# The feed-forward's first projection by Strassen's scheme

## The chip, the cores and the metric

One core of a Trainium2 chip runs the whole program as one launch. The metric is the device time in microseconds (us). The engines are TensorE (PE, which multiplies matrices into PSUM; PEld is its weight load), VectorE (DVE), ScalarE (ACT), GpSimd (POOL) and SyncE (SP, which issues nearly all DMAs). Each takes its own instructions in a fixed order; semaphores hold one engine for another.

## The reference

Two transformer blocks follow each other on 1024 tokens of width 1024. Only the second one's feed-forward is touched, with the step just ahead of it:

```
x = x + merged @ w_out
h2 = rmsnorm(x, g_ffn)
u = causal_dwconv(h2 @ w_up, conv_w, conv_b)        # w_up: 1024 x 5632, three taps over tokens
x = x + (gelu(u[..., :2816]) * u[..., 2816:]) @ w_down
ple_gate = sigmoid(rmsnorm(x, g_ple) @ w_ple_gate)
x = x + ple_gate * (p @ w_ple_up)
```

All is float32. The feed-forward's width of 2816 is 22 tiles of 128 features, each a gate tile i and a value tile i + 22.

## The kernel before

Activations lie with features on the 128 partitions and tokens along the row. A float32 product is made of three passes: each factor is split into a high part (rounded to the PE's fp32r format) and a low part, and high by high, high by low and low by high are added up in PSUM (`mm3`, line 223 for every matmul). Weights come in by SP's queue, ACT copies the high part, DVE subtracts it for the low part (`split`, lines 271 and 272); `weight` keeps two raw tiles and four of each part.

`merge` ends with `product(j, f)`, one output tile f of half j of the tokens (512 each): 24 matmuls, then DVE adds the residual (line 1821). After the third tile of the second half, `norm(0)` normalises the first half: squares on ACT, their sum mostly on POOL (line 448), a root by small matmuls, then for each of 8 tiles a scaling on DVE (line 475), the high part (477) and the low part (478). `norm(1)` does the same at the end.

`ffn` takes the 22 activations in groups of 4, 4, 4, 4 and 6. For one activation, `ffn_act` multiplies the gate and the value tile of `w_up` with both halves, 48 matmuls into two PSUM banks each; ACT scales straight from PSUM by the last tap (line 1933), DVE adds the two other taps, again from PSUM (line 1936), ACT takes gelu (1938), POOL multiplies (1939), and the product is split. It stays in SBUF. After each group `down` adds that group's share of all 8 output tiles into `xacc` (line 1858), while the next group's first activation is prepared. Then the last stage multiplies by `w_ple_gate`.

The order of instructions on each engine is chosen by the framework's scheduler: by the order of the program, filled up with what its own cost estimates say is ready.

Of the kernel before, what the change touches and what calls it, by code (L numbers as in the profile page):

```python
# [17 lines left out]
P = 128  # L18
# [19 lines left out]
FF_GROUPS = (4, 4, 4, 4, 6)  # L38
# [178 lines left out]
class _Builder:  # L217
# [123 lines left out]
    def build(self):  # L341
        nc, tc, a = self.nc, self.tc, self.a
        with ExitStack() as es:
# [1442 lines left out]
    def merge(self):  # L1786
# [4 lines left out]
        with tc.tile_pool(name="merge", bufs=1, reuse_waits="tile") as pool:  # L1791
# [21 lines left out]
            for j, t in enumerate(half):  # L1813
                X = self.hp.tile([P, KT, 512], F32, tag="h", name="x")
                nc.sync.dma_start(out=X, in_=src[:, t].rearrange("(k p) t -> p k t", p=P))
                xs.append(X)
            def product(j, f):
# [3 lines left out]
                nc.vector.tensor_tensor(out=xs[j][:, f, :], in0=ps, in1=xs[j][:, f, :], op=ALU.add)  # L1821

            def norm(j):
                t = half[j]
                if self.stop == "m":
                    self.store(a["out"][:, t].rearrange("(k p) t -> p k t", p=P), xs[j])
                self.store(dst[:, t].rearrange("(k p) t -> p k t", p=P), xs[j])
                h = self.h_tiles(512)
                self.norm(pool, xs[j], 512, lambda f: self.vec("g_ffn", f), None, h[0], h[1])
                hs.append(h)  # L1830

            for f in range(KT):
                product(0, f)
            for f in range(KT):
                product(1, f)
                if f == 2:
                    norm(0)
            norm(1)
        return hs

    def ffn(self, hs):
        nc, tc, a = self.nc, self.tc, self.a
        with tc.tile_pool(name="ffn", bufs=1, reuse_waits="tile") as big:
            X = big.tile([P, KT, SEQ], F32, name="xacc")
            for j in range(2):
                nc.sync.dma_start(out=X[:, :, 512 * j:512 * j + 512], in_=self.xd[0][:, 512 * j:512 * j + 512].rearrange("(k p) t -> p k t", p=P))
# [19 lines left out]
            with tc.tile_pool(name="ffa", bufs=1, reuse_waits="tile") as pool:  # L1866
                u_t = self.hp.tile([P, 4, SEQ], F32, tag="h", name="u")
                act = lambda i: self.ffn_act(pool, hs, i, u_t[:, 2 * (i % 2):2 * (i % 2) + 2])
                first, acts = 0, []
                for gn in FF_GROUPS:  # L1870
                    acts += [act(first + i) for i in range(len(acts), gn)]
                    ahead = [act(first + gn)] if first + gn < FFT else []
                    weight = lambda f: self.weight(a["w_down"][f][:, first * P:(first + gn) * P])
                    if ahead:
                        for f in range(KT):
                            w = weight(f)
                            for j in range(2):
# [78 lines left out]
```

## Time and profile before

| | us |
|---|---|
| median of 3 runs | 4063.01 (4056.43 to 4072.8) |
| the profiled execution | 4071.35 |
| its span | 4069.6 |
| PE busy | 3755.1 |
| DVE busy | 2386.8 |
| ACT busy | 1612.1 |
| POOL busy | 929.7 |

The feed-forward runs from about 3211 to 3950 us of the span. A matmul's recorded 0.39 us overlaps with the next one's, so PE's pace is read from how many start in a window, not from the mean of one.

### The profile page before, as it was taken

What the parts mean: (1) busy time and instruction counts of PE and PEld (TensorE: products, weight loads), DVE (VectorE), ACT (ScalarE), POOL (GpSimd) and SP (SyncE); (2) the same over time, 40 slices, a digit from 0 to 9 for tenths busy, and PEclk for the clock granted to TensorE, in tenths of its full rate; (3) what the DMA queues carried; (4) which work ended last, traced back from release to release, by engine and by line L of the source; (5) the groups of instructions that cost most, each with busy time, mean ns of one, the idle gap of its engine ahead of it and who ended that gap; (6) DMA issues with size and microseconds to landing.
All of it is one profiled execution on the core that took longest, in us unless ns stands there. A gap on an engine that the chain in (4) does not pass through costs nothing. (4 is left out here: it accounts for less than half of the span.)

```text
span 4069.6 us, 52648 instructions
## 1 busy us (share of the span) xinstructions
PE 3755.1 (92%) x18392; PEld 2809.5 (69%) x18392; DVE 2386.8 (59%) x5500; ACT 1612.1 (40%) x3251; POOL 929.7 (23%) x1127
## 2 busy tenths in 40 slices
PE   5899999888899999799999989989869999999999
PEld 4755666566755666478778866666648788888877
DVE  5888755645787747655664337776544543434354
ACT  4445663334346653543333234443343422222243
POOL 3233322311233324311110023343312100000020
PEclk8999999989999999899999978998879999999999
DMA  5111126564111135543333242121224411111133
GB/s 179 46 43 42 55 88 188 188 215 147 39 42 40 56 129 191 166 129 89 108 100 102 87 115 55 47 69 23 68 100 143 149 50 47 50 47 47 49 92 105
DMA packets 267890, 379.20 MB, mean 93 GB/s; under 512 B 56400, under 2 KB 145440, under 8 KB 264024
## 3 DMA queue, kind: packets, MB, share of 16 engines
q1 hardware_dynamic: 267624, 375.83, 29.8%
q8 instruction: 146, 2.39, 0.3%
q14 instruction: 120, 0.98, 0.1%
HBM read 280.90 MB, written 87.54 MB: 91 GB/s over the span
## 5 line engine op out<-in xcount | busy, mean ns | idle before, releaser
L223 PE MATMUL pp<-h,wh 128*128 128x512 f32 (+1 forms) x1696 | 527.3, 388 | 50.6 <-DVE x L1148 16.9
L223 PE MATMUL pp<-wh,h 128*128 128x384 f32 (+1 forms) x1792 | 518.2, 352 | 15.4 <-ACT v L548 12.6
L272 DVE TENSOR_TENSOR wl<-wr,wh 128x512 fp32r<-128x512 f32 (+3 forms) x386 | 299.7, 781 | 393.4 <-ACT wh L271 391.6
L223 PE MATMUL dd<-h,wh 128*128 128x512 f32 x1664 | 519.5, 393 | 0.0
L271 ACT CAST wh<-wr 128x512 fp32r<-128x512 f32 (+3 forms) x386 | 249.9, 651 | 611.3 <-PE pp L223 286.7
L223 PEld LDWEIGHTS pp<-h,wh 128*128 128x128 f32 x1696 | 315.7, 194 | 128.9 <-ACT wh L271 17.8
L709 POOL TENSOR_TENSOR acc<-acc,p 128x512 f32<-128x512 f32 (+3 forms) x246 | 295.3, 1200 | 443.3 <-ACT p L694 275.7
L223 PEld LDWEIGHTS dd<-h,wh 128*128 128x128 f32 x1664 | 312.5, 188 | 71.4 <-DVE h L478 0.3
L223 PEld LDWEIGHTS pp<-wh,h 128*128 128x128 f32 x1792 | 335.2, 194 | 34.0 <-ACT v L548 13.9
L223 PE MATMUL rp<-h,side 128*128 128x512 f32 x1440 | 350.6, 396 | 0.0
L223 PE MATMUL pp<-h,wl 128*128 128x512 f32 (+1 forms) x848 | 327.1, 386 | 1.0 <-DVE wl L272 0.9
L223 PE MATMUL dd<-h,wl 128*128 128x512 f32 x832 | 325.9, 392 | 0.0
L223 PE MATMUL pp<-wl,h 128*128 128x384 f32 (+1 forms) x896 | 312.6, 349 | 0.0
L223 PE MATMUL sp<-q,k 66*128 66x512 f32 (+6 forms) x944 | 300.1, 407 | 11.2 <-DVE p L692 5.7
L223 PEld LDWEIGHTS rp<-h,side 128*128 128x128 f32 x1440 | 266.5, 189 | 52.0
L634 DVE TENSOR_REDUCE mx<-mp 128x1 f32<-128x512 f32 (+1 forms) x472 | 250.7, 559 | 55.3 <-PE mp L223 53.4
L223 PE MATMUL mp<-k,q 128*128 128x512 f32 (+3 forms) x664 | 232.5, 383 | 13.5 <-DVE mx L634 6.4
L709 DVE TENSOR_TENSOR acc<-acc,p 128x512 f32<-128x512 f32 (+3 forms) x246 | 201.1, 817 | 68.0 <-ACT p L694 26.8
L223 PEld LDWEIGHTS sp<-q,k 128*128 128x128 f32 (+1 forms) x944 | 164.0, 192 | 108.7 <-issue 55.7
L694 ACT ACTIVATE p<-sp 128x512 f32<-128x512 f32 (+1 forms) x316 | 181.4, 594 | 141.3 <-PE sp L223 128.1
L223 PE MATMUL pp<-act,wh 128*128 128x512 f32 x704 | 221.4, 396 | 2.0 <-ACT act L271 1.1
L223 PE MATMUL vp<-p,v 128*64 128x512 f32 (+3 forms) x824 | 212.9, 596 | 5.5 <-ACT p L694 5.1
(371 smaller groups left out, 6705.5 us busy)
## 6 DMA issues: line engine op xcount, KB each, us to landing
wr<-in_w_out SPq DMA_DIRECT2D x96, 256.0 KB
wr<-in_w_up SPq DMA_DIRECT2D x88, 256.0 KB
wmod<-in_w_mod SPq DMA_DIRECT2D x16, 1024.0 KB
wr<-in_w_tok SPq DMA_DIRECT2D x40, 384.0 KB
xd<-x SPq DMA_DIRECT2D x6, 2048.0 KB
wr<-in_w_feat SPq DMA_DIRECT2D x40, 256.0 KB
bq<-in_na_bias SPq DMA_DIRECT2D x16, 640.0 KB
yd<-yr SPq DMA_DIRECT2D x32, 256.0 KB
```

Of the source, the lines that this page charges most:

```text
L223: return self.nc.tensor.matmul(out, lhsT=lhsT, rhs=rhs, start=start, stop=stop)
L271: self.nc.scalar.copy(out=hi, in_=src)
L272: self.nc.vector.tensor_tensor(out=lo, in0=src, in1=hi.bitcast(F32), op=ALU.subtract)
L634: nc.vector.tensor_reduce(out=m, in_=ps[:, :n], axis=AX.X, op=ALU.max)
L694: made = nc.scalar.activation(out=p[:, j, :n], in_=st[:, :n], func=AF.Exp)
L709: u.summed = eng.tensor_tensor(out=u.acc[:, j, q0:q0 + n], in0=u.acc[:, j, q0:q0 + n], in1=p[:, j, :n], op=ALU.add)
```

## The change

One gate and one value tile, with both halves of the inner dimension, form a 2 x 2 block matrix; the two halves of the features and of the tokens form the other. The four block products of 128 by 512 by 512 each have two terms, eight multiplications; the change makes seven, by Winograd's form of Strassen's scheme. It needs sums of blocks on both sides:

- The tokens' side, once: `norm_here` scales both halves in place, and `turn_b` forms four difference blocks t1 to t4 on DVE and POOL, each split. `merge` now adds up the squares as the tiles come, alternately on DVE and POOL, spreads the first half's norm over the second half's products, and stores the residual by ACT's queue.
- The weights' side, per pair: `blocks` loads both tiles and makes four sums on POOL; `operand` splits each of the seven operands, four products ahead.
- The results: `tile_pair` adds the seven products up, partly from PSUM on DVE, partly on POOL, into z in SBUF; the convolution reads z from there. Its steps are laid out by a table of product numbers, and from product 14 on the order is kept as written (`pin`).

PSUM is one ring of eight banks in this stage. All 22 activations are written to DRAM by ACT's queue and read back by SP's queue for `down`, which now has groups of 4 and six times 3; the last two groups run for the first half of the tokens, then for the second.

```
-FF_GROUPS = (4, 4, 4, 4, 6)
+FF_GROUPS = (4, 3, 3, 3, 3, 3, 3)
+PIN = 14
+AHEAD = 4
...
+    def pin(self, op):
+        return (lambda **k: self.tc.keep_in_program_order(op(**k))) if self.pinned else op
...
-            with self.weights("second"), self.psum("dense", pp=2, tp=1, vp=1, dd=2):
-                hs = self.merge()
-                if self.stop == "m":
-                    return
-                self.ffn(hs)
+            with tc.tile_pool(name="factor", bufs=1) as fp:
+                with self.weights("second"), self.psum("merge", pp=2, tp=1, vp=1):
+                    hs = self.merge(fp)
+                    if self.stop == "m":
+                        return
+                with self.psum("up", pp=8):
+                    self.up(*hs)
+            with tc.tile_pool(name="x", bufs=1, reuse_waits="tile") as xp, self.weights("third"):
+                with self.psum("dense", pp=2, tp=1, vp=1, dd=2):
+                    self.ffn(xp.tile([P, KT, SEQ], F32, name="xacc"))
...
+    def norm_here(self, X, gain, r, first, hi, lo, fs):
+        for f in fs:
+            self.nc.vector.scalar_tensor_tensor(out=X[:, f], in0=X[:, f], scalar=gain(f), in1=r, op0=ALU.mult, op1=ALU.mult)
+            if f >= first:
+                self.split(X[:, f], hi[:, f - first], lo[:, f - first])
...
+            sums, here = [None, None], self.norm_tile(pool)
+            tile = lambda tag: fp.tile([P, 512], F32, tag=tag, name=tag) if tag == "nr" else here(tag)
...
+                nc.scalar.dma_start(out=(a["out"] if self.stop == "m" else dst)[f * P:(f + 1) * P, half[j]], in_=xs[j][:, f])
+            def add(j, f):
+                sums[j] = self.norm_sum(xs[j], 512, nc.gpsimd if f % 2 else nc.vector, tile, (f,), sums[j])
...
+                    t = self.hp.tile([P, 2, 4, 512], F32R, tag="h", name="h22")
+                    h = [t[:, 0], t[:, 1]]
...
+                r = self.norm_root(pool, sums[j], 512, tile)
+                return [lambda f=f: self.norm_here(xs[j], lambda k: self.vec("g_ffn", k), r, 4 * j, *h, range(f, f + 2)) for f in ((0, 2, 4, 6) if j == 0 else (4, 6, 0, 2))]
...
+                if f == 1:
+                    todo = norm(0)
+                elif todo:
+                    todo.pop(0)()
+                if f >= 3:
+                    for k in range(4) if f == 3 else (f,):
+                        add(1, k)
+            last = norm(1)
+        return hs, xs, last
...
+            def diff(eng, t, k, out, x, y):
+                eng.tensor_tensor(out=out, in0=x, in1=y, op=ALU.subtract)
+                self.split(out, t[0][:, k], t[1][:, k])
+            def turn_b():
+                x0, x1 = ([X[:, k] for k in range(KT)] for X in xs)
+                for k in range(4):
+                    diff(V, t1, k, x0[k], x1[k], x0[k])
+                for k in range(4):
+                    G.tensor_tensor(out=x1[k], in0=x1[k + 4], in1=x1[k], op=ALU.subtract)
+                    diff(V, t2, k, x1[k + 4], x1[k + 4], x0[k])
+                for k in range(4):
+                    self.split(x1[k], t3[0][:, k], t3[1][:, k])
+                    diff(G, t4, k, x0[k + 4], x0[k + 4], x1[k + 4])
+            z_t = self.hp.tile([P, 4, SEQ], F32, tag="h", name="z")
+            act_t = self.hp.tile([P, 2, 2, SEQ], F32R, tag="h", name="act")
+            z, u = z_t[:, 0:2], z_t[:, 2:4]
+            left, right = slice(0, 512), slice(512, 1024)
+            held = lambda: pool.tile([P, 512], F32, tag="held", name="held", bufs=4)
...
+            def blocks(i):
+                raw = []
+                for s in range(2):
+                    t = pool.tile([P, 2, 512], F32, tag="raw", name="raw", bufs=4)
+                    nc.sync.dma_start(out=t.rearrange("p k c -> p (k c)"), in_=a["w_up"][i + FFT * s])
+                    raw += [t[:, 0], t[:, 1]]
+                a11, a12, a21, a22 = raw
+                s1, s2 = (pool.tile([P, 512], F32, tag="sum", name="sum", bufs=4) for _ in range(2))
+                self.pin(G.tensor_tensor)(out=s1, in0=a21, in1=a22, op=ALU.add)
+                self.pin(G.tensor_tensor)(out=s2, in0=s1, in1=a11, op=ALU.subtract)
+                self.pin(G.tensor_tensor)(out=a21, in0=a11, in1=a21, op=ALU.subtract)
+                s4 = lambda: self.pin(G.tensor_tensor)(out=a12, in0=a12, in1=s2, op=ALU.subtract)
+                return [a11, a12, s1, s2, a21, a22, a12], s4
...
+            def lower():
+                src, t = operand.last
+                ins = self.pin(V.tensor_tensor)(out=t[:, 1], in0=src, in1=t[:, 0].bitcast(F32), op=ALU.subtract)
+                operand.done = operand.done[0], ins
...
+            order = [(0, 0), (0, 1), (1, 0), (1, 1), (0, 6), (1, 6)]
+            order += [(i, j) for i in range(FFT) for j in range(7) if (i, j) not in order]
+            got = {}
+            def operand(n):
+                if n < len(order):
+                    i, j = order[n]
+                    if i not in got:
+                        got[i] = blocks(i)
+                    if j == 5 and i >= 1 and i + 1 < FFT:
+                        got[i + 1] = blocks(i + 1)
+                    src = got[i][0][j]
+                    t = pool.tile([P, 2, 512], F32R, tag="op", name="op", bufs=6)
+                    copied = self.pin(A.copy)(out=t[:, 0], in_=src)
+                    operand.done = copied, operand.done[1]
+                if n and n <= len(order):
+                    if n != AHEAD:
+                        lower()
+                    i, j = order[n - 1]
+                    if j == 1:
+                        got[i][1]()
+                if n < len(order):
+                    operand.last = src, t
+                    ops.append(t)
...
+            of_b = (b11, b21, t1, t2, t3, t4, b22)
+            def product(n):
+                operand(n + AHEAD)
+                b, w, ps = of_b[order[n][1]], ops.pop(0), self.bank()
+                for k in range(4):
+                    c = slice(k * P, (k + 1) * P)
+                    for i, (x, y) in enumerate(((0, 0), (0, 1), (1, 0))):
+                        self.mm(ps, w[:, x, c], b[y][:, k], k + i == 0, k == 3 and i == 2)
+                return ps
...
+            def convolve(i, s):
+                self.pin(A.activation)(out=u[:, s], in_=z[:, s], func=AF.Identity, scale=taps(i, s)(2), bias=self.vec("conv_b", i + FFT * s))
+                def rest():
+                    for n in (1, 0):
+                        d = 2 - n
+                        self.pin(V.scalar_tensor_tensor)(out=u[:, s, d:], in0=z[:, s, :SEQ - d], scalar=taps(i, s)(n), in1=u[:, s, d:], op0=ALU.mult, op1=ALU.add)
+                return rest
...
+            def tile_pair(i):
+                add = lambda eng, out, x, y: self.pin(eng.tensor_tensor)(out=out, in0=x, in1=y, op=ALU.add)
+                act, b, at, rest = act_t[:, i % 2], made[i], {}, {}
+                p, v, uv = held(), held(), held()
+                def put(n, fn):
+                    at.setdefault(n, []).append(fn)
+                put(1, lambda: self.pin(A.copy)(out=p, in_=b[0]))
+                put(2, lambda: add(V, z[:, 0, left], b[1], p))
+                put(3, lambda: self.pin(A.copy)(out=v, in_=b[2]))
+                put(4, lambda: add(V, p, b[3], p))
+                put(4, lambda: add(G, uv, p, v))
+                put(5, lambda: add(V, p, b[4], p))
+                put(5, lambda: add(G, z[:, 1, right], p, v))
+                put(6, lambda: add(V, z[:, 1, left], b[5], p))
+                put(7, lambda: add(V, z[:, 0, right], b[6], uv))
+                put(7, lambda: rest.update(x=convolve(i, 1)))
+                put(8, lambda: rest["x"]())
+                put(8, lambda: rest.update(y=convolve(i, 0)))
+                put(9, lambda: rest["y"]())
+                put(10, lambda: self.pin(A.activation)(out=u[:, 0], in_=u[:, 0], func=AF.Gelu_apprx_tanh))
+                put(11, lambda: self.pin(G.tensor_tensor)(out=u[:, 0], in0=u[:, 0], in1=u[:, 1], op=ALU.mult))
+                put(13, lambda: self.pin(A.copy)(out=act[:, 0], in_=u[:, 0]))
+                put(14, lambda: self.pin(V.tensor_tensor)(out=act[:, 1], in0=u[:, 0], in1=act[:, 0].bitcast(F32), op=ALU.subtract))
+                put(15, lambda: self.pin(nc.scalar.dma_start)(out=self.ad[i], in_=act.bitcast(F32)))
+                first = 7 * i + 4
+                todo.extend((first + n, fn) for n in sorted(at) for fn in at[n])
...
+            with tc.issue_after(operand.done[0].ins), tc.issue_after(operand.done[1].ins):
+                for fn in norm:
+                    fn()
+                turn_b()
+            for n, (i, j) in enumerate(order):
+                self.pinned = n >= PIN
+                if j == (2 if i < 2 else 0):
+                    tile_pair(i)
+                made[i][j] = product(n)
+                run(n)
...
+                if i % 2 == 0:
+                    t = self.hp.tile([P, 2, 2, SEQ], F32R, tag="h", name="acts")
+                nc.sync.dma_start(out=t[:, i % 2].bitcast(F32), in_=self.ad[i])
+                self.acts.append(t[:, i % 2])
...
+                def load(i):
+                    t = pool.tile([P, 2, SEQ], F32R, tag="act", name="act", bufs=6)
+                    nc.sync.dma_start(out=t.bitcast(F32), in_=self.ad[i])
+                    return t
+                starts = [sum(FF_GROUPS[:n]) for n in range(len(FF_GROUPS))]
+                weight = lambda n, f: self.weight(a["w_down"][f][:, starts[n] * P:(starts[n] + FF_GROUPS[n]) * P])
+                acts = {0: self.acts}
+                for n in range(len(FF_GROUPS) - 2):
+                    acts[n + 1] = []
+                    for f in range(KT):
+                        w = weight(n, f)
+                        if n == 0:
+                            nc.sync.dma_start(out=X[:, f], in_=self.xd[0][f * P:(f + 1) * P, 0:SEQ])
+                        if f % 2 and f // 2 < FF_GROUPS[n + 1]:
+                            acts[n + 1].append(load(starts[n + 1] + f // 2))
+                        for j in range(2):
+                            down(acts[n], w, f, j, range(FF_GROUPS[n]))
+                todo = []
+                for j in range(2):
+                    for n in (-2, -1):
+                        n += len(FF_GROUPS)
                         for f in range(KT):
-                            w = weight(f)
-                            for j in range(2):
-                                down(acts, w, f, j, range(gn))
-                    else:
-                        w = [weight(f) for f in range(2)]
-                        for ks in (range(gn - 1), range(gn - 1, gn)):
-                            for f in range(2):
-                                down(acts, w[f], f, 0, ks)
-                        for f in range(2, KT):
-                            down(acts, weight(f), f, 0, range(gn))
-                        todo = norm(0)
-                        for f in range(KT):
-                            w = weight(f)
+                            w = weight(n, f)
+                            if j == 0 and n + 1 < len(FF_GROUPS) and f % 2 and f // 2 < FF_GROUPS[n + 1]:
+                                acts.setdefault(n + 1, []).append(load(starts[n + 1] + f // 2))
                             if todo:
                                 todo.pop(0)()
-                            down(acts, w, f, 1, range(gn))
-                    first += gn
-                    acts = ahead
+                            down(acts[n], w, f, j, range(FF_GROUPS[n]))
...
-    def ffn_act(self, pool, hs, i, u):
```

## Rows read from the trace of the kernel before

**Rows 1.** The page's header, busy times and slices of the span.
```profile
span 4069.6 us, 52648 instructions
...
PE 3755.1 (92%) x18392; PEld 2809.5 (69%) x18392; DVE 2386.8 (59%) x5500; ACT 1612.1 (40%) x3251; POOL 929.7 (23%) x1127
...
PE   5899999888899999799999989989869999999999
...
PEclk8999999989999999899999978998879999999999
```

**Rows 2.** Windows: stretch, us, PE, PEld, DVE, ACT, POOL busy (instructions), PEclk, DMA share, GB/s.
```profile
3150.00:3200.00 50.00, 46.25 (x204) 37.59 (x203) 27.93 (x44) 19.57 (x32) 9.08 (x6) 0.97 0.35 116
...
3300.00:3350.00 50.00, 50.00 (x218) 40.72 (x217) 23.25 (x27) 12.21 (x16) 4.79 (x2) 1.00 0.18 51
...
3850.00:3900.00 50.00, 48.03 (x201) 38.21 (x199) 21.00 (x22) 16.67 (x21) 7.77 (x4) 0.97 0.25 72
```

**Rows 3.** Timeline of PE in merge: start, us, engine, line, operation, idle before.
```profile
3192.70 0.77 PE L223 MATMUL pp<-m21h,wh 128*128 128x512 f32 x1 [3.75 <-ACT h L477]
...
3194.12 0.63 PE L223 MATMUL pp<-m21h,wh 128*128 128x512 f32 x1
3194.55 0.63 PE L223 MATMUL pp<-m21l,wh 128*128 128x512 f32 x1
```

**Rows 4.** Groups by line and shape, 3000 to 4070: count, busy us, mean ns, idle, releasers.
```profile
L272 DVE TENSOR_TENSOR wl<-wr,wh 128x512 fp32r<-128x512 f32 x196 | 142.2, 727 | 263.9 <-ACT wh L271 263.6
...
L271 ACT CAST wh<-wr 128x512 fp32r<-128x512 f32 x196 | 121.1, 619 | 402.2 <-PE dd L223 196.8 <-PE pp L223 173.9 <-DMA wr<-in_w_out 14.4
...
L1936 DVE SCALAR_TENSOR_TENSOR u<-dd,vecs,u 128x1023 f32<-128x1023 f32 x44 | 56.5, 1283 | 21.6 <-ACT u L1933 21.5
...
L1858 DVE TENSOR_TENSOR xacc<-pp,xacc 128x512 f32<-128x512 f32 x80 | 55.2, 691 | 117.0 <-PE pp L223 116.9
L1933 ACT ACTIVATE u<-dd,vecs 128x1024 f32<-128x1024 f32 x44 | 52.9, 1202 | 1.9 <-PE dd L223 1.9
L1939 POOL TENSOR_TENSOR u<-u 128x1024 f32<-128x1024 f32 x22 | 52.6, 2392 | 622.1 <-DVE u L1936 602.2 <-DMA wr<-in_w_down 20.0
...
L272 DVE TENSOR_TENSOR act<-u,act 128x1024 fp32r<-128x1024 f32 x22 | 27.0, 1226 | 67.9 <-ACT act L271 67.9
...
L271 ACT CAST act<-u 128x1024 fp32r<-128x1024 f32 x22 | 23.1, 1049 | 98.7 <-POOL u L1939 98.7
...
L475 DVE SCALAR_TENSOR_TENSOR y<-x,vecs,nr 128x512 f32<-128x512 f32 x16 | 11.1, 746 | 3.9 <-ACT nr L462 3.9
```

**Rows 5.** Timelines of POOL, then of DVE, where both work.
```profile
3191.37 1.72 POOL L448 TENSOR_TENSOR nrb<-nrb,y 128x512 f32<-128x512 f32 x1 [34.58 <-ACT y L446]
3193.83 4.95 POOL L448 TENSOR_TENSOR nrb<-nrb,y 128x512 f32<-128x512 f32 x3 [0.74 <-ACT y L446]
3203.26 1.29 POOL L448 TENSOR_TENSOR nrb<-nrb,y 128x512 f32<-128x512 f32 x1 [4.49 <-ACT y L446]
...
3329.47 2.40 POOL L1939 TENSOR_TENSOR u<-u 128x1024 f32<-128x1024 f32 x1 [20.31 <-DVE u L1936]
```
```profile
3191.87 0.68 DVE L1821 TENSOR_TENSOR x<-pp,x 128x512 f32<-128x512 f32 x1
...
3194.76 2.87 DVE L272 TENSOR_TENSOR wl<-wr,wh 128x512 fp32r<-128x512 f32 x2
...
3330.86 1.57 DVE L272 TENSOR_TENSOR wl<-wr,wh 128x512 fp32r<-128x512 f32 x1
```

**Rows 6.** Timeline of DVE from merge's last addition to the second norm's first scaling.
```profile
3211.01 0.69 DVE L1821 TENSOR_TENSOR x<-pp,x 128x512 f32<-128x512 f32 x1
3212.42 0.69 DVE L272 TENSOR_TENSOR wl<-wr,wh 128x512 fp32r<-128x512 f32 x1 [0.72 <-ACT wh L271]
...
3218.53 2.08 DVE L475 SCALAR_TENSOR_TENSOR y<-x,vecs,nr 128x512 f32<-128x512 f32 x3 [1.93 <-ACT nr L462]
```

**Rows 7.** Windows in which two 2 MB loads move.
```profile
3230.00:3235.00 5.00, 5.00 (x24) 4.10 (x23) 3.73 (x4) 2.74 (x4) 0.00 (x0) 1.00 1.04 376
```

More of the change, by code (lines that the diff above doesn't have):

```diff
@@ L1784, in rwkv, with merge @@
                         nc.sync.dma_start(out=a["out"][f * P:(f + 1) * P, 256 * j:256 * j + 256], in_=o)
-    def merge(self):
+    def merge(self, fp):
         nc, tc, a = self.nc, self.tc, self.a
@@ L1827, in norm @@
-                self.store(dst[:, t].rearrange("(k p) t -> p k t", p=P), xs[j])
-                h = self.h_tiles(512)
-                self.norm(pool, xs[j], 512, lambda f: self.vec("g_ffn", f), None, h[0], h[1])
+                if j == 0:
+                    h = self.h_tiles(512)
+                else:
+                    t = self.hp.tile([P, 2, 4, 512], F32R, tag="h", name="h22")
+                    h = [t[:, 0], t[:, 1]]
                 hs.append(h)
+                r = self.norm_root(pool, sums[j], 512, tile)
@@ L1832, in merge @@
+                return [lambda f=f: self.norm_here(xs[j], lambda k: self.vec("g_ffn", k), r, 4 * j, *h, range(f, f + 2)) for f in ((0, 2, 4, 6) if j == 0 else (4, 6, 0, 2))]
             for f in range(KT):
                 product(0, f)
+                add(0, f)
+            todo = []
             for f in range(KT):
                 product(1, f)
[L1836 to L1841, printed above, removed]
+                if f == 1:
[5 more added lines that the diff above has]
+                        add(1, k)
@@ new lines, in merge, with up, taps, run @@
+            last = norm(1)
+        return hs, xs, last
+    def up(self, hs, xs, norm):
+        nc, tc, a = self.nc, self.tc, self.a
+        V, G, A = nc.vector, nc.gpsimd, nc.scalar
+        self.pinned = False
+        self.ad = self.dp.tile([FFT, P, 2, SEQ], F32, name="ad")
+        with tc.tile_pool(name="up", bufs=1, reuse_waits="tile") as pool:
+            def diff(eng, t, k, out, x, y):
[16 more added lines that the diff above has]
+            held = lambda: pool.tile([P, 512], F32, tag="held", name="held", bufs=4)
+            ts = {n: pool.tile([P, 2, 4, 512], F32R, name="t%d" % n) for n in (4, 3)}
+            def blocks(i):
[11 more added lines that the diff above has]
+                return [a11, a12, s1, s2, a21, a22, a12], s4
+            ops = []
+            def lower():
[25 more added lines that the diff above has]
+                    ops.append(t)
+            operand.done = None, None
+            for n in range(AHEAD):
+                operand(n)
+            lower()
+            ts.update({n: pool.tile([P, 2, 4, 512], F32R, name="t%d" % n) for n in (1, 2)})
+            b11, b21, b22 = [x[:, 0:4] for x in hs[0]], [x[:, 4:8] for x in hs[0]], hs[1]
+            t1, t2, t3, t4 = ([ts[n][:, 0], ts[n][:, 1]] for n in range(1, 5))
+            of_b = (b11, b21, t1, t2, t3, t4, b22)
[7 more added lines that the diff above has]
+                return ps
+            def taps(i, s):
+                return lambda n: self.vec("conv_w", 2 * FFT * n + i + FFT * s)
+            def convolve(i, s):
[5 more added lines that the diff above has]
+                return rest
+            todo = []
+            def run(n):
+                for x in [x for x in todo if x[0] <= n]:
+                    todo.remove(x)
+                    x[1]()
+            def tile_pair(i):
[24 more added lines that the diff above has]
+                todo.extend((first + n, fn) for n in sorted(at) for fn in at[n])
+            made = [[None] * 7 for _ in range(FFT)]
+            with tc.issue_after(operand.done[0].ins), tc.issue_after(operand.done[1].ins):
[8 more added lines that the diff above has]
+                run(n)
+            self.acts = []
+            for i in range(FF_GROUPS[0]):
+                if i % 2 == 0:
+                    t = self.hp.tile([P, 2, 2, SEQ], F32R, tag="h", name="acts")
+                nc.sync.dma_start(out=t[:, i % 2].bitcast(F32), in_=self.ad[i])
+                self.acts.append(t[:, i % 2])
+            for n in range(len(order), len(order) + 24):
+                run(n)
@@ L1893, in ffn @@
-                    first += gn
-                    acts = ahead
+                            down(acts[n], w, f, j, range(FF_GROUPS[n]))
+                    if j == 0:
+                        todo = norm(0)
             if self.stop == "f":
```

34 lines of the change are left out of this document (2 added, 32 removed).

## The prediction

> **What bounds the kernel now.** I read the page's busy table and slices first: TensorE (PE) is busy 92% of a 4069.6 us span, and in the last quarter of the slices it is full but for a tenth here and there, at a clock of 9 tenths or more [rows 1]. The windows say it harder: across the feed-forward a 50 us window holds 50.00 us of PE, 218 matmuls and clock 1.00, while VectorE (DVE) is busy 23 us, ScalarE (ACT) 12 and GpSimd (POOL) 5 [rows 2]. So this stage runs at PE's pace, 50 / 218 = 0.229 us per matmul of 512 columns, and only two places lose some: 3150 to 3200 (PE 46.25, clock 0.97) and 3850 to 3900 (48.03, 0.97). The first is a wait of 3.75 us of PE behind the norm of the first half, followed by matmuls at 0.43 us apart for some 3 us, that is at 1.2 GHz [rows 3]. Every other engine is hidden under PE here. The question is whether that still holds when PE's work shrinks by an eighth and that of DVE and POOL grows.
>
> **What is removed.** The up-projection has 44 tiles of 48 matmuls, 2112 x 0.229 = 483.6 us. Afterwards it has 154 block products of 12, 1848 x 0.229 = 423.2 us: 60.4 us of PE go. The down-projection keeps its 22 x 8 x 2 x 3 = 1056.
>
> **What is added per pair of tiles** (one pair of gate and value tiles gives seven products; PE needs 84 x 0.229 = 19.2 us). Durations are from [rows 4]:
> - DVE: 7 low parts of operands, 0.69 each where POOL is idle [rows 6], 4.8; 5 additions of a product from PSUM at 0.69, 3.5; 4 convolution taps of 1023 columns at 1.28, 5.1; the low part of the activation 1.23. Sum 14.6 us (before: four low parts, four taps, one 1.23, 9.1).
> - POOL: 4 sums of weight blocks and 2 of products at 1.29 [rows 5], 7.7, and the gating product 2.39. Sum 10.1 us (before 2.4).
> - ACT: 9 copies at 0.62, 2 scalings at 1.20, gelu and high part taken at 1.05 each. Sum 10.1 us; hidden.
>
> Alone, each lies below 19.2. But DVE and POOL don't run beside each other freely. In [rows 5] POOL multiplies from 3329.47 to 3331.87; a DVE low part that starts at 3330.86 takes 1.57 us where 0.69 is usual and ends 0.56 us after POOL. Two of them at 3194.76 take 2.87 us under three POOL additions, which themselves take 1.65 each for 1.29. Yet a DVE addition that takes one input from PSUM keeps its 0.68 under a running POOL addition (3191.87). What shuts the other out is two SBUF inputs. Now the change does two things at once: it multiplies POOL's work by four, and its taps read z from SBUF, where before they read PSUM; so of DVE's 14.6 us, 4.8 + 5.1 + 1.2 = 11.2 (76%) are of the kind that waits.
>
> What a POOL operation costs DVE: all but the start of both, which overlaps (0.69 - 0.56 = 0.13 us on DVE, about as much on POOL), so 1.0 us for one of 512 columns and 2.1 for the gating product (the parts that exclude one another add up to 11.2 + 10.1 - 19 x 0.13 = 18.8 us of a pair). That is 6 x 1.0 + 2.1 = 8.1 us per pair when every one meets such a DVE operation, 0.76 x 8.1 = 6.2 when they meet in proportion. DVE then needs 20.8 to 22.7 us per pair, more than PE's 19.2. Below lies only the case that they never meet, 19.2. I take 21.3: the proportion, and half a us because DVE works in order and waits for ACT (before, 67.9 us in 22 waits for the activation's high part alone [rows 4]). So DVE, not PE, sets the pace of the up-projection.
>
> The Trainium skill ("SBUF — State Buffer", section "Who interferes with whom") speaks against the change here: a DVE instruction with two SBUF inputs and a GpSimd one that reads SBUF share one lock, and the second to issue is blocked for the whole instruction. The rows agree on who blocks whom, not on the whole instruction: by that the lock alone would be held 21.3 us per pair and bind by itself (2 us a pair above PE's pace even with DVE's PSUM additions free; that the figure is the one I took is chance), while by the rows the starts overlap.
>
> **Head of the up-projection.** After merge's last matmul the chain of the second norm took 3211.01 to 3218.53 before the first scaled column, 7.5 us [rows 6]; its last addition is moved to POOL (1.29 for 0.69), so 8.1. Before, PE filled this with the first half's matmuls. Now DVE has 8 scalings at 0.746, 20 low parts and 8 differences at 0.69: 25.3 us, and 8 differences on POOL cost it some 7 more, before the last of Strassen's token blocks stands: 8.1 + 25.3 + 7 = 40.4 us. PE can do ten products in 27.5 us by then, so it is late by 13 even if nothing else binds.
>
> DVE's account to the last product: 40.4 + 22 x 21.3, less 7 low parts that fit into the chain's gaps (4.8), less what it does after the last product (additions 2.1, taps 5.1, 1.2, the gating product 2.1: 10.5) = 493.7 us, against 483.6: **+10.1**. Ends: 20.8 gives -1, 22.7 gives +41, PE's pace with the late head 423.2 + 13 gives -47.
>
> **Turn to the down-projection.** Its first four activations (4 MB) can load once the first half's tiles are free, five products (15 us) ahead of the end; two 2 MB loads moved 376 GB/s [rows 7], so 11 us: hidden. What isn't is DVE's 10.5 us rest, behind which the two PSUM banks' additions and the first weights' low parts stand. I take **+6** (0 to 15). A gap here and one at the head each end in some matmuls at half clock, as the gap in merge did [rows 3], where it cost 0.03 x 50 = 1.5 us [rows 2]: **+3**.
>
> **The down-projection.** Seven groups for five: 112 additions for 80, each 0.69 under 9 matmuls (2.06 us), and one low part of 384 columns per two of them, under the 0.73 of 512: at most 2.1 of 4.1 us, hidden by PE; uncovered it would be 32 x 0.69 = 22 us. The activations' writes go over ACT's queue, 1 MB in 21 us; the reads stand in SP's queue ahead of weights, 2.7 us per MB, and the slowest group needs 9 MB in 44 us, 205 GB/s, half of what was seen. I take **+2** (0 to 12) for weights that arrive late behind an activation that itself waits for a buffer; DVE, then PE stand behind such a weight.
>
> **What goes.** The norm of the first half is cut into steps between products, so the 3.75 us wait and its slow clock, 5 us, should go; and the last group no longer waits for the last activation, 50 - 201 x 0.229 = 4.0 us, of which I count 3.7 [rows 2]: **-8.7**. What is late next there is the second half's norm, which the head above carries. Moving the residual's stores, sixteen of 256 KB, from SP's queue to ACT's costs nothing: ACT is busy a quarter of the feed-forward's windows, and nothing waits for the stores before the down-projection.
>
> **Sum**: +10.1 + 6 + 3 + 2 - 8.7 = +12.4 on the profiled execution's 4071.35, 4084; that execution lies 8.3 above the median of the runs, 4063.01, so 4076 against that.
>
> **Rivals.** (a) PE stays the bound: the queues run far enough ahead that POOL's operations fall beside DVE's PSUM additions and gaps. For it: the 18.8 us that exclude one another fit under 19.2, operands are made four products ahead, eight PSUM banks. Against: each engine's order is fixed, and 98% use of what two engines share, with no queueing, is much to ask. -47 + 6 + 3 + 2 - 8.7 = -45: 4018. (b) Slower: every POOL operation stops DVE, in the steady part of the up-projection, because DVE is never idle and its next operation is nearly always a two-input one (12 of 17). Price 22.7 per pair, +41 for +10: 4106. From 21.6 us per pair on the whole is over 0.5% slower. For it: the two low parts under three POOL additions, where all met. Against: ACT's waits let POOL work alone at times. (c) The round trip through DRAM binds: activations wait for buffers in SP's queue, six groups lose 5 us each where I counted 2 in all: 4104. Against: 376 GB/s and a whole group of lead. That fewer products are computed than said can't be: they are counted in the code.
>
> **Chances.** About 0.5% (20 us) is what a measurement of this kernel can tell from no change. Forecast 0.42, (a) 0.31, (b) 0.22, (c) 0.05. The forecast's own range is 4052 to 4096; since (a) has a third, the whole range takes it in, down to 4010 (its sum with the turn at nothing and the reads at nothing), and reaches up almost to (b), 4104. Faster than 4043: (a) nearly whole, 0.30. Over 4083: (b), (c) all but whole and a tail of the forecast, 0.30. Between: 0.40.
>
> **What would show it.** Matmuls fall by 264. In windows of the up-projection DVE would be near 50 of 50 with low parts of a mean well over 0.69 and taps over 1.28, PE near 45, its waits ended by DVE's low parts; a new group of matmuls should begin every 21 us per pair. If PE stands at 50.00 there and DVE's taps at 1.28, (a) is right and the exclusion was overrated. If PE waits for activations or weights in the last 260 us of that stage, it is (c). The head should show PE idle 10 us or more behind low parts of token blocks.

## The result, and the profile after

The changed kernel took 4090.47 us in the median (4083.16 to 4096.25, 6 runs) against 4066.30 of the kernel before beside it (4056.43 to 4072.8, 6 runs): a ratio of 1.0067, 95% interval 1.0047 to 1.0087. It is slower by 0.7%. The rise is 24 us where 12.4 were forecast; the time lies inside the range given, above the 4083 over which the prediction had put 0.30. That range is wide, so the time alone says little for the mechanism; the rows below say more.

The page's header, busy times and two rows of slices, of the kernel after, as [rows 1] of before:

```profile
span 4093.2 us, 52895 instructions
...
PE 3702.4 (90%) x18128; PEld 2760.2 (67%) x18128; DVE 2667.7 (65%) x5756; ACT 1675.9 (41%) x3395; POOL 1184.5 (29%) x1263
...
PE   5899999888899999799999989999869799998999
...
PEclk7999999989999999899999978998979899999999
```

PE lost 264 matmuls and 53 us of work, and the span grew all the same. Windows of merge and of the up-projection, columns as in [rows 2]:

```profile
3150.00:3200.00 50.00, 50.00 (x226) 40.94 (x225) 30.98 (x49) 21.09 (x35) 5.22 (x4) 1.00 0.44 143
...
3300.00:3350.00 50.00, 47.53 (x202) 38.55 (x202) 47.18 (x40) 22.80 (x32) 31.18 (x16) 0.97 0.23 85
3450.00:3500.00 50.00, 43.60 (x185) 34.89 (x184) 47.15 (x40) 22.12 (x32) 31.92 (x16) 0.97 0.23 85
```

In merge the wait of [rows 3] is gone: PE is at 50.00 where 46.25 stood. In the up-projection, where PE filled 50 of 50 before, DVE is the engine with almost no idle time now. Groups of DVE, then of POOL, from 3300 to 3650 us (count, busy us, mean ns, idle, releaser), beside [rows 4]:

```profile
L242 DVE TENSOR_TENSOR op<-raw,op 128x512 fp32r<-128x512 f32 x81 | 100.6, 1242 | 0.0
L242 DVE SCALAR_TENSOR_TENSOR z<-z,vecs 128x1022 f32<-128x1022 f32 x33 | 72.5, 2196 | 1.2
L242 DVE SCALAR_TENSOR_TENSOR z<-z,vecs 128x1023 f32<-128x1023 f32 x32 | 57.3, 1790 | 0.0
L242 DVE TENSOR_TENSOR z<-pp,held 128x512 f32<-128x512 f32 x49 | 33.6, 685 | 1.8
L242 DVE TENSOR_TENSOR held<-pp,held 128x512 f32<-128x512 f32 x32 | 21.9, 685 | 18.9 <-POOL held L242 18.9
```
```profile
L242 POOL TENSOR_TENSOR raw<-raw 128x512 f32<-128x512 f32 x17 | 38.5, 2265 | 0.0
L242 POOL TENSOR_TENSOR sum<-raw 128x512 f32<-128x512 f32 x16 | 36.3, 2267 | 0.0
```

In the mean a low part takes 1.24 us for 0.69, a tap 2.20 or 1.79 for 1.28, a POOL sum of these two groups 2.27 for 1.29; the two groups with one input in PSUM stay at 0.685. The means mix long and short ones: of the low parts in the first row 48 take 0.68, 16 take 1.18 and 17 take 2.89, and of the taps with 1023 columns half take 1.27 and half 2.31. (The line L242 is the helper that keeps an order.) How the two engines take turns shows in their timelines, DVE first, then POOL:

```profile
3400.01 3.51 DVE L242 SCALAR_TENSOR_TENSOR z<-z,vecs 128x1023 f32<-128x1023 f32 x2
3403.44 1.77 DVE L242 TENSOR_TENSOR op<-sum,op 128x512 fp32r<-128x512 f32 x1
...
3410.98 2.88 DVE L242 TENSOR_TENSOR op<-raw,op 128x512 fp32r<-128x512 f32 x1
...
3421.50 3.51 DVE L242 SCALAR_TENSOR_TENSOR z<-z,vecs 128x1023 f32<-128x1023 f32 x2
```
```profile
3400.23 2.21 POOL L242 TENSOR_TENSOR raw<-raw,sum 128x512 f32<-128x512 f32 x1 [3.03 <-DVE op L242]
3402.40 2.26 POOL L242 TENSOR_TENSOR sum<-raw 128x512 f32<-128x512 f32 x1
...
3410.90 2.42 POOL L242 TENSOR_TENSOR z<-z 128x1024 f32<-128x1024 f32 x1 [2.31 <-ACT z L242]
```

Each ends about its own length after the other has ended: the second POOL sum ends at 3404.66, the low part that started under it ends at 3405.21, 0.55 later. The low part of 2.88 us stands under the gating product. The Trainium skill ("SBUF — State Buffer", section "Who interferes with whom") has this as a lock that whoever issues first holds for the whole instruction; the rows agree but for the start of each, some 0.14 us, which overlaps.

What PE waits for in the same stretch (us, times, longest):

```profile
PEld pp L225 <- DVE z L242: 31.2, 16, 2.6
PE pp L225 <- DVE z L242: 24.4, 16, 2.2
```

DVE's additions of products into z come late, so no PSUM bank is free for the next product. A pair takes 21.50 us on DVE once the pace is steady: the first taps of two pairs start at 3400.01 and 3421.50. By the starts of PE's products the mean from the fourth pair to the 21st is 21.24, because two of these 17 spacings, 19.04 and 19.63, are of the time before the backlog.

The stage account of all kernels, in us of each profiled execution. "Up" runs from merge's last addition on DVE to the start of the last product's last matmul; "turn" from there to the down-projection's first; "down" from there to the first matmul of the stage after. "Pair" is the steady spacing. (The kernel before alternates between up and down, so only its sum is given.)

| kernel | pair | up | turn | down | sum |
|---|---|---|---|---|---|
| before | | | | | 739.5 |
| after | 21.50 | 498.2 | 11.1 | 262.3 | 771.6 |
| e1_all_on_vector | 19.04 | 457.6 | 3.9 | 262.1 | 723.6 |
| e2_write_only | 19.04 | 454.1 | 3.8 | 261.7 | 719.5 |
| e3_sums_on_vector | 20.20 | 472.7 | 11.8 | 262.1 | 746.6 |
| e7_weight_sums_on_gpsimd | 20.18 | 473.8 | 7.6 | 261.9 | 743.3 |
| e4_last_pass_joined | 21.50 | 498.1 | 11.2 | 250.5 | 759.7 |
| e5_vector_and_joined | 19.04 | 457.5 | 3.8 | 250.5 | 711.8 |
| e6_and_token_differences | 19.04 | 453.5 | 3.7 | 250.3 | 707.6 |
| e8_six_operands_ahead | 19.04 | 448.1 | 3.7 | 250.5 | 702.3 |

From before to after these stages grow by 32.1; merge's last addition stands 8.2 earlier (3211.01 to 3202.84: the forecast's 5, and 3.4 of scatter ahead of merge), the stage after is the same within 0.4. That is the 23.6 us between the two profiled executions (4095.0 and 4071.35). Single executions scatter more than some effects below: merge's last addition stands at 3190.50 in e1 and 3204.20 in e8, with the same code up to there. So small effects are read from the stages, one trace for each kernel.

### The profile page after: what moved, and what is told of

It is laid out like the page before. It is cut to its first block, busy times and chain, and to the rows that moved or that the text cites. A ratio compares the mean times of both kernels' runs of the same rounds, so it can differ in the third digit from the quotient of the medians.

```text
span 4093.2 us, 52895 instructions
## 1 busy us (share of the span) xinstructions
PE 3702.4 (90%) x18128; PEld 2760.2 (67%) x18128; DVE 2667.7 (65%) x5756; ACT 1675.9 (41%) x3395; POOL 1184.5 (29%) x1263
## 5 line engine op out<-in xcount | busy, mean ns | idle before, releaser
L277 ACT CAST wh<-wr 128x512 fp32r<-128x512 f32 (+4 forms) x322 | 199.7, 625 | 428.0 <-PE pp L225 258.2
L278 DVE TENSOR_TENSOR wl<-wr,wh 128x512 fp32r<-128x512 f32 (+4 forms) x322 | 240.0, 751 | 192.3 <-ACT wh L277 190.1
L225 PEld LDWEIGHTS pp<-wh,h 128*128 128x128 f32 x1792 | 333.2, 193 | 35.4 <-ACT v L566 14.7
L225 PE MATMUL sp<-q,k 66*128 66x512 f32 (+6 forms) x944 | 299.1, 406 | 11.2 <-DVE p L710 5.9
L225 PE MATMUL pp<-t,op 128*128 128x512 f32 x1056 | 256.2, 402 | 41.6 <-DVE z L242 26.6
L225 PEld LDWEIGHTS pp<-t,op 128*128 128x128 f32 x1056 | 203.0, 194 | 94.1 <-DVE z L242 33.8
L225 PE MATMUL mp<-k,q 128*128 128x512 f32 (+3 forms) x664 | 231.9, 382 | 14.6 <-DVE mx L652 6.2
L459 POOL TENSOR_TENSOR nrb<-nrb,y 128x512 f32<-128x512 f32 (+1 forms) x52 | 67.7, 1302 | 501.8 <-ACT y L457 485.4
L225 PEld LDWEIGHTS mp<-k,q 128*128 128x128 f32 x664 | 119.7, 189 | 123.9 <-DVE mx L652 54.4
```

What stands on the lines that cost most here:

```text
L225: return self.nc.tensor.matmul(out, lhsT=lhsT, rhs=rhs, start=start, stop=stop)
L277: self.nc.scalar.copy(out=hi, in_=src)
L278: self.nc.vector.tensor_tensor(out=lo, in0=src, in1=hi.bitcast(F32), op=ALU.subtract)
L459: (add or (nc.vector if f == KT - 1 else nc.gpsimd)).tensor_tensor(out=rb[:, :n], in0=rb[:, :n], in1=sq[:, :n], op=ALU.add)
```

## The experiments

The theory: POOL's operations and DVE's with two SBUF inputs exclude each other, and this makes DVE the bound. e1 to e4 ran beside one set of runs of before (median 4060.21, 13 runs), e5 to e8 beside another (4061.44, 17 runs).

**e1_all_on_vector.** All seven POOL operations of a pair go to DVE, the busiest engine of the stage.

```
-self.pin(G.tensor_tensor)(out=s1, in0=a21, in1=a22, op=ALU.add)
+self.pin(V.tensor_tensor)(out=s1, in0=a21, in1=a22, op=ALU.add)
...
-put(4, lambda: add(G, uv, p, v))
+put(4, lambda: add(V, uv, p, v))
...
-put(11, lambda: self.pin(G.tensor_tensor)(out=u[:, 0], in0=u[:, 0], in1=u[:, 1], op=ALU.mult))
+put(11, lambda: self.pin(V.tensor_tensor)(out=u[:, 0], in0=u[:, 0], in1=u[:, 1], op=ALU.mult))
```

> GpSimd's seven operations per pair (four sums of weight blocks, two of products, the gating product) are given to VectorE; nothing else changes. Theory (VectorE sets the pace, and a GpSimd operation that reads SBUF costs a two-SBUF-input VectorE operation about 1.0 us of 1.29): VectorE then needs 14.6 + 6 x 0.69 + 1.23 = 20.0 us per pair, low parts back to 0.69 and taps to 1.28, against 21.24 before: 20 to 27 us less, about 4066, although the busiest engine gets 5.4 us more work per pair. Rival 1 (VectorE is simply given too much, the exclusion adds little): its busy 19.9 us per pair grows by 5.4 to 25.3, 22 x 4.1 = 89 us more, 4180. Rival 2 (the order of the queues and PSUM banks set the pace): no change, 4090.

Measured: 4041.64 us (4035.4 to 4047.94), ratio to before 0.9955 (0.994 to 0.997): 1.1% below the changed kernel's ratio, some 45 us, and below the kernel before. A window and three DVE groups of this kernel:

```profile
3300.00:3350.00 50.00, 50.00 (x223) 41.40 (x222) 48.85 (x65) 23.66 (x34) 0.00 (x0) 1.00 0.27 101
```
```profile
L242 DVE TENSOR_TENSOR op<-raw,op 128x512 fp32r<-128x512 f32 x88 | 60.2, 684 | 0.0
L242 DVE SCALAR_TENSOR_TENSOR z<-z,vecs 128x1023 f32<-128x1023 f32 x38 | 48.5, 1277 | 0.0
...
L242 DVE TENSOR_TENSOR raw<-raw,sum 128x512 f32<-128x512 f32 x17 | 11.8, 692 | 0.6
```

With seven operations more DVE is done sooner: 18.62 us busy per pair, low parts and taps back at their own length, and PE is the bound at 19.04. I had expected 20.0 for DVE from summed durations. Its operations run closer together than they last, in the timeline of this kernel 0.60 us apart at 0.68 each:

```profile
3202.34 0.68 DVE L1928 TENSOR_TENSOR raw<-raw 128x512 f32<-128x512 f32 x1
3202.95 0.68 DVE L1929 TENSOR_TENSOR raw<-raw,sum 128x512 f32<-128x512 f32 x1
3203.55 0.68 DVE L1936 TENSOR_TENSOR op<-raw,op 128x512 fp32r<-128x512 f32 x1
```

**e2_write_only.** Each POOL operation becomes two memsets of the same tile, so that POOL stays busy but reads nothing. The sums, the gating product and with them the values are left out.

```
+w = lambda out: [self.pin(G.memset)(ap=out, constant=0.01) for _ in range(2)]
...
-self.pin(G.tensor_tensor)(out=s1, in0=a21, in1=a22, op=ALU.add)
+w(s1)
...
-put(4, lambda: add(G, uv, p, v))
+put(4, lambda: w(uv))
```

> Each of GpSimd's seven operations per pair is replaced by two memsets of the same output tile, so GpSimd still works but reads nothing; the sums, the gating product and with them the values are left out. Theory (what excludes is GpSimd reading SBUF beside a VectorE operation with two SBUF inputs): low parts at 0.69, taps at 1.28, TensorE's 19.2 us per pair sets the pace, about 41 us less, 4050. Rival 1 (any GpSimd activity holds VectorE up): low parts and taps stay well above that in proportion to GpSimd's busy time, and the pace stays above 20.5. Rival 2 (VectorE's own 14.6 us and its waits in order set the pace): durations fall, the pace stays near 21.

Measured: 4037.58 us (2 runs), ratio 0.9945 (0.9925 to 0.9965). A window, and one group each of POOL and DVE:

```profile
3300.00:3350.00 50.00, 50.00 (x222) 41.38 (x222) 35.05 (x45) 23.89 (x33) 19.78 (x34) 1.00 0.29 106
```
```profile
L242 POOL MEMSET raw<- 128x512 f32 x61 | 32.1, 527 | 106.9 <-DVE op L242 105.2
```
```profile
L242 DVE TENSOR_TENSOR op<-raw,op 128x512 fp32r<-128x512 f32 x80 | 55.2, 690 | 68.4 <-ACT op L242 68.4
```

POOL is still busy 20 us of 50, and DVE's low parts stay at 0.69 and its taps at 1.28. They do meet: here a low part starts under a memset that runs until 3400.63, and keeps its 0.69.

```profile
3399.68 0.95 POOL L242 MEMSET z<- 128x1024 f32 x1
```
```profile
3400.41 0.69 DVE L242 TENSOR_TENSOR op<-raw,op 128x512 fp32r<-128x512 f32 x1 [1.43 <-ACT op L242]
```

So it is POOL's reading that holds DVE, not its being busy. The Trainium skill ("SBUF — State Buffer", section "Who interferes with whom") has this too: two SBUF inputs contend with a GpSimd instruction that reads SBUF, not with one that only writes it. DVE's own work of a pair, measured bare here, is 13.88 us. The stages fall by 52 us where 41 were expected for the pace: up by 44, the turn by 7.

**e3_sums_on_vector.** Only the four weight sums go to DVE (the edit of e1, `s1`, `s2`, `a21` and `s4` alone).

> Only the four sums of weight blocks per pair go from GpSimd to VectorE; the two sums of products and the gating product stay. Theory: VectorE 14.6 + 4 x 0.69 = 17.4, plus 0.76 x (2 x 1.0 + 2.1) = 3.1 for what GpSimd still does: 20.5 us per pair, 0.75 x 22 = 16 us less than the changed kernel, 4074. Rival (too much on VectorE): 19.9 + 2.8 = 22.7 per pair, 32 us more, 4122.

Measured: 4065.58 us (4055.13 to 4070.37, 10 runs), ratio 1.0004 (0.9992 to 1.0016), about half of what e1 gains over the changed kernel. The first nine pairs come at 19.04, the rest at 20.20. Two groups from 3450 to 3650 us:

```profile
L242 DVE TENSOR_TENSOR op<-raw,op 128x512 fp32r<-128x512 f32 x49 | 38.3, 782 | 0.0
L242 DVE TENSOR_TENSOR sum<-raw 128x512 f32<-128x512 f32 x10 | 28.9, 2892 | 0.0
```

Each time the same sum stands under POOL's gating product and takes 2.9 us: which operations meet is fixed by the written order, not by chance.

**e7_weight_sums_on_gpsimd.** The mirror: the weight sums stay on POOL, the other three go to DVE.

```
-put(4, lambda: add(G, uv, p, v))
+put(4, lambda: add(V, uv, p, v))
...
-put(5, lambda: add(G, z[:, 1, right], p, v))
+put(5, lambda: add(V, z[:, 1, right], p, v))
...
-put(11, lambda: self.pin(G.tensor_tensor)(out=u[:, 0], in0=u[:, 0], in1=u[:, 1], op=ALU.mult))
+put(11, lambda: self.pin(V.tensor_tensor)(out=u[:, 0], in0=u[:, 0], in1=u[:, 1], op=ALU.mult))
```

> The mirror of the kernel with only the weight sums on VectorE: here the four weight sums stay on GpSimd, and the two product sums and the gating product go to VectorE. Theory: a price per operation. VectorE's busy 18.62 us of a pair with all seven, less four sums at 0.60 is 16.2; each sum on GpSimd stops VectorE for up to 1.0, so up to 20.2, at the share that the changed kernel had (21.24 less 13.8 over 8.1, 0.92) 19.9 us per pair; the time is some 20 us over the kernel with all on VectorE, about that of the kernel before. Rival: only the long gating product and the product sums, which stand in the chain from products to activation, cost time; the weight sums are made a pair ahead and fall beside additions from PSUM, so the pace is PE's 19.04 and the time that of all on VectorE, -18 against before.

Measured: 4063.34 us (4057.21 to 4069.18, 10 runs), ratio 1.0005 (0.9995 to 1.0015); 19.90 us per pair in the mean and 20.18 once steady. The price per operation held, the rival fell. That the mean meets the expected 19.9 is chance: the pairs come at 19.04 first and at 20.18 later, where every sum costs its full price. Groups from 3450 to 3650 us:

```profile
L242 DVE SCALAR_TENSOR_TENSOR z<-z,vecs 128x1022 f32<-128x1022 f32 x20 | 44.0, 2199 | 0.7
L242 DVE SCALAR_TENSOR_TENSOR z<-z,vecs 128x1023 f32<-128x1023 f32 x20 | 35.8, 1791 | 0.0
L242 DVE TENSOR_TENSOR op<-raw,op 128x512 fp32r<-128x512 f32 x49 | 33.5, 683 | 0.0
L242 DVE TENSOR_TENSOR op<-sum,op 128x512 fp32r<-128x512 f32 x20 | 24.5, 1226 | 0.0
```

By these means the four sums cost 2 x 0.92 + 2 x 0.51 + 2 x 0.54 = 3.9 us of a pair, 1.0 for each sum. One by one they land on three of the four taps (2.20, 2.31, 2.20 us) and on one of the two low parts of sums (1.77, the other 0.68); the five low parts of raw blocks are untouched. Taps and low parts of sums have the same lengths in the changed kernel; there the low parts of raw blocks are stretched besides, by POOL's other operations.

**e4_last_pass_joined.** For the second half of the tokens the last two groups of the down-projection become one of six activations, 18 matmuls for each weight instead of 9 twice.

```
-for n in (-2, -1):
+for n in (-2, -1) if j == 0 else (-1,):
...
-w = weight(n, f)
+w = weight(n, f) if j == 0 else self.weight(a["w_down"][f][:, starts[-2] * P:])
...
-down(acts[n], w, f, j, range(FF_GROUPS[n]))
+ks = acts[n] if j == 0 else acts[n - 1] + acts[n]
+down(ks, w, f, j, range(len(ks)))
```

> In the down-projection's last pass (second half of the tokens) the last two groups of three are multiplied with one weight of six tiles, 18 matmuls for 9, as the kernel before had it. Theory (there TensorE waits for weights that come every 9 matmuls, 2.06 us, beside the norm's steps): the 8 us lost between 3937 and 3962 fall to 2 or 3, 5 us less, 4085. Rival (the norm's own steps on ScalarE and VectorE hold TensorE there): no change.

Measured: 4079.36 us (4074.08 to 4083.29, 4 runs), ratio 1.0047 (1.0032 to 1.0062) where the changed kernel had 1.0067; the traces put the stage 11.8 us below, where 5 were expected. The last 50 us ahead of the stage after, of the changed kernel and of this one:

```profile
3924.40:3974.40 50.00, 41.11 (x180) 30.89 (x179) 37.62 (x63) 25.11 (x45) 13.63 (x11) 1.00 0.34 99
```
```profile
3902.90:3952.90 50.00, 49.48 (x222) 39.90 (x222) 37.61 (x58) 26.83 (x44) 11.32 (x9) 1.00 0.39 119
```

So the change lost most of its 12 us here (42 matmuls fewer in 50 us, 9.6 us at 0.229), with the clock at 1.00: weights that serve nine matmuls, norm steps beside them, and the first matmul of the stage after behind both. What PE's weight loads wait for most in this stretch of the changed kernel are the norm's high parts on ACT (us, times, longest):

```profile
PEld pp L225 <- ACT h L488: 4.5, 3, 2.6
```

They are gone in e4. That the weights' transfers are late is not enough: ACT waits for them 9.1 us in this stretch and 8.2 in e4's. How much is the norm steps' and how much the short products' isn't told apart, since e4 gives PE more cover against both.

**e5_vector_and_joined.** e1 and e4 together.

> All seven GpSimd operations of a pair on VectorE, and the last two groups of the down-projection joined to one of six activations for the second half of the tokens. Theory: the two gains lie in different stages and add up. The first alone was 18.6 us below the kernel before, the second alone took 11.1 off the changed kernel, so -29.7 against before in the same job (4030 if before stands at 4060); the pace stays at 19.04 us per pair, the down-projection goes from 257.5 to some 247 to 250 us. Rival: the norm steps in the last pass, not the nine-matmul weights, hold PE there; with GpSimd out of the way in the stage before, nothing changes in this one, but the two could meet in the wait at the turn: only -5 more than the first alone, -24.

Measured: 4028.78 us (4018.4 to 4038.62), ratio 0.9918 (0.9901 to 0.9935), 33 us under before; the traces' sum falls by 11.8 from e1's. The two add up.

**e6_and_token_differences.** e5, with the eight token differences that POOL made at the head on DVE too.

```
-G.tensor_tensor(out=x1[k], in0=x1[k + 4], in1=x1[k], op=ALU.subtract)
+V.tensor_tensor(out=x1[k], in0=x1[k + 4], in1=x1[k], op=ALU.subtract)
...
-diff(G, t4, k, x0[k + 4], x0[k + 4], x1[k + 4])
+diff(V, t4, k, x0[k + 4], x0[k + 4], x1[k + 4])
```

> As the kernel with both, and the eight differences of token blocks that GpSimd makes at the head go to VectorE too. Theory: VectorE sets the length of the head, where PE stands still for 25.1 us; GpSimd's 8 differences took 13.7 us there and cost VectorE what 31 us of its stretch are over 8 scalings, 20 low parts and 8 differences back to back (8 x 0.68 + 28 x 0.60 = 22.2), that is 9; on VectorE they cost 8 x 0.60 = 4.8. So PE's gap shrinks to some 21 us and the time falls by 4. Rival: the low parts overlap with GpSimd's differences well enough, and eight more operations on the engine that is late there lengthen the gap by 4.8.

Measured: 4022.71 us (4020.57 to 4036.37), ratio 0.9912 (0.9895 to 0.9928). The medians don't tell it from e5; the traces do: "up" is 4.0 shorter, PE's long stop at the head 20.4 us for 25.0.

**e8_six_operands_ahead.** e6, with six operands for four made ahead of the norm.

```
-for n in range(AHEAD):
+for n in range(AHEAD + 2):
     operand(n)
...
-operand(n + AHEAD)
+if n >= 2:
+    operand(n + AHEAD)
```

> As the kernel with the token differences on VectorE, and six operands for four are made before the norm and the token blocks, so that PE has six products for its idle stretch at the head. Theory: PE is the bound after the head, so each product of 2.7 us done in the idle stretch is one less behind it: -5.4, less the two operands' low parts and one weight sum that now stand ahead of the first scaling (3 x 0.60 = 1.8): -3.6. Rival: the fifth and sixth product were in time anyway, since they need the second half's own block, which is ready ten us later, and the later scalings push the token blocks back: +1.8.

Measured: 4025.26 us (4014.65 to 4028.62), ratio 0.9903 (0.9887 to 0.992); again only the trace tells it from e6, "up" 5.4 shorter. Groups of PE at the head of this kernel (start, length, count, idle before):

```profile
3213.52 19.03 PE L225 MATMUL pp<-h,op 128*128 128x512 f32 x72 [1.19 <-ACT op L1953]
3232.39 0.97 PE L225 MATMUL pp<-t,op 128*128 128x512 f32 x2
...
3249.71 12.63 PE L225 MATMUL pp<-t,op 128*128 128x512 f32 x48 [7.63 <-DVE op L1936]
```

Six products (72 matmuls) run where four did. The rival was right that the token blocks come later: the low part of the last one ends 46.7 us after merge's last addition, for 44.3 in e6. PE gains all the same: its longest stop is 7.6 us for 20.4. This version beats both kernels, by 1.0% the one before.

## Why the prediction was right, and where it was not

**DVE sets the pace: shown.** These signs named for it came: 264 matmuls fewer, DVE at 47 of 50, long low parts and taps, 21.50 us per pair for 21.3. e1 and e2 show the cause from two sides. One sign was wrong: PE's waits end with DVE's additions into z, not with low parts. The operands are early; the PSUM banks come free late.

**The 21.3 is made of three terms, and two sizes were off against each other.** DVE's own work: 14.6 forecast, 13.88 measured (e2), since operations follow one another faster than they last. Exclusion: 6.2 forecast "in proportion"; DVE is busy 20.14 of a steady pair in the changed kernel, 6.3 above its own work. Waiting: "half a us because DVE works in order and waits for ACT"; it is 21.50 - 20.14 = 1.36, of which 18.9 / 16 = 1.2 is not for ACT but for POOL: DVE writes p in place and must wait until POOL's sum has read it. The price of 1.0 per POOL operation held in e7 (3.9 for four). Proportion was not the mechanism, and that it came to nearly the measured 6.3 is luck: the written order decides what meets. The four weight sums pay in full, so does the gating product (a low part of 2.89 for 0.69), and the two product sums lengthen DVE's operations by 0.5 between them (the low part of 1.18).

**Rival (a)** describes e1, not this kernel: with POOL's work gone PE is the bound, and the time is 4041.64. **Rival (b)**, 22.7 per pair, was too much by 1.2. **Rival (c)** is refuted for the activations' reads: from 3750 to 3900 us PE is at 50.00 in every window, the last of them

```profile
3850.00:3900.00 50.00, 50.00 (x218) 40.76 (x217) 22.37 (x37) 6.19 (x13) 0.00 (x0) 1.00 0.45 160
```

**Head: right in kind, short in size.** The last token block's low part ended 49.6 us after merge's last addition (3252.4 less 3202.84), for 40.4. DVE's timeline of the changed kernel:

```profile
3207.70 0.79 DVE L258 TENSOR_TENSOR rsu<-rsv,rsr 128x4 f32<-128x4 f32 x1
3208.52 1.19 DVE L259 SCALAR_TENSOR_TENSOR rsu<-rsu,rsr 128x4 f32<-128x4 f32 x1
...
3213.80 3.58 DVE L1936 TENSOR_TENSOR op<-raw,op 128x512 fp32r<-128x512 f32 x4 [3.37 <-ACT op L1953]
3217.30 5.18 DVE L501 SCALAR_TENSOR_TENSOR x<-x,vecs,nr 128x512 f32<-128x512 f32 x3
```

The chain to the first scaling took 14.5 for 8.1: POOL's first weight sums hold two operations of four columns (0.16 each in e1), and the first four low parts stand ahead of the scaling, where the forecast had them "fit into the chain's gaps". The rest took 35.1 for 32.3. "Up" is only 4.5 over the forecast's 493.7: the first pairs after the head still run at PE's 19.04 (three of them, then one at 19.63), which gives back some 8 us, while 21.50 for 21.3 in the others costs some 3.

**Turn: 11.1 for 6.** The cover named was DVE's rest; what PE waits for is ACT (10.8 us in one wait). ACT's timeline of the changed kernel:

```profile
3708.70 1.24 ACT L242 ACTIVATE z<-z,vecs 128x1024 f32<-128x1024 f32 x1 [2.26 <-POOL z L242]
...
3710.38 1.24 ACT L242 ACTIVATE z<-z,vecs 128x1024 f32<-128x1024 f32 x1 [0.44 <-DVE z L242]
3711.53 1.12 ACT L277 CAST wh<-wr 128x512 fp32r<-128x512 f32 x2
```

The first weights' high parts stand behind two scalings that wait for POOL and DVE; with POOL out of it the turn is 3.9 (e1). Some matmuls at half clock follow it, as forecast (PEclk 0.86 from 3700 to 3750).

**The term furthest off is the down-projection's: "-3.7" for the last group's wait, with "+2" for the reads.** Down has 1056 x 0.229 = 241.8 us of matmuls and took 262.3, 20.5 over; before, the stages lost 739.5 - 725.4 = 14.1 in all. The wait itself went, as forecast. In the kernel before PE stood behind the last activation's high part from 3840 to 3960:

```profile
PEld pp L223 <- ACT act L271: 1.5, 1, 1.5
```

In the kernel after no wait of PE for an activation is left from 3890 to 4000. But the new last pass brings 12 us of its own, which e4 takes away. The forecast priced seven groups for five by DVE's additions and never looked at the last pass, where a weight serves one half of the tokens only. Over these stages the forecast was 739.5 + 17.4 = 756.9 and the measured sum is 771.6, 14.7 over: up +4.5, turn and clock some +2, down +8. The wait in merge came as forecast (-5, 4.8 measured), and the 3.4 us of scatter ahead of merge hide part of this: the profiled executions differ by 23.6 where 12.4 were forecast.

## What to carry to other kernels

Before work goes to GpSimd to spare VectorE, count which VectorE operations read two SBUF tiles: each GpSimd operation that reads SBUF and meets one of them costs VectorE most of its own length (1.0 us of 1.29 here) where doing it itself costs 0.6. Reduced matmuls pay only to the pace of the next engine, so add up that engine's work by spacing, not by recorded length, and include waits for tiles overwritten in place. Price the head, the turn and the last pass separately: here the turn and the last pass cost 11 and 12 us, each about as much as the whole rise that was forecast.

## What the runs showed of the hardware that was not expected

- VectorE operations of 512 float32 that are recorded as 0.68 us follow each other every 0.60; summed lengths overstated its work of a pair by 0.7 us (14.6 for 13.88).
- GpSimd's memsets (0.527 us for 512 columns) left VectorE's two-input operations at 0.69 while GpSimd was busy 40% of the time.
- VectorE's smallest operations, four columns wide, went from 0.16 to 0.79 and 1.19 us under GpSimd's sums: the price goes by GpSimd's length, not by VectorE's.
- With PE waiting once in each pair the granted clock was 0.97 in most windows; with the same matmuls and no waits it was 1.00 (e1).
